# Low products on VectorE alone, and an eviction that runs key by key, in the spreading of the experts' weights of a PEER block

## The chip, the cores and the metric

One NeuronCore of a Trainium2 chip runs the whole program. The metric is the device time of one execution in microseconds; three executions of the kernel before gave 1767.48, 1770.31 and 1774.57 us, a median of 1770.31 us. The engines are TensorE (PE, with its weight loads PEld), VectorE (DVE), ScalarE (ACT), GpSimd (POOL) and the DMA queue of SyncE (SP). Each engine takes its instructions in the order in which they stand in its queue and waits on semaphores for the others.

## The reference, cut to what matters

The program is one decoder block: a token mixer (gated MLP and window attention), and then PEER, a layer that picks experts out of 128 x 128 = 16384 single-neuron experts. For each of 512 tokens and 8 heads it takes the 16 best pairs of a first and a second key, a softmax over their scores, and sums the chosen experts:

```python
e = (take_along_axis(i1, ci // 16) * 128 + take_along_axis(i2, ci % 16))
g = softmax(sc)
act = gelu(einsum('thkd,td->thk', peer_u[e], xb))
return einsum('thk,thkd->td', g * act, peer_v[e])
```

A token thus has 8 x 16 = 128 picks, each with a first key, a second key and a weight g.

## The kernel before, in words

For the first 384 tokens (three blocks of 128; `DENSE = 3`) the kernel computes all 16384 experts densely instead of gathering them: a U chunk is the product of the tokens with 128 experts' rows of `peer_u` (`U_chunk`, 128 chunks of 24 matmuls of 128x384: 8 slices of the model width times three products of hi and lo parts, lines 63 to 65), followed by GELU; a V chunk multiplies the activations by the experts' weights and by rows of `peer_v` and adds into six PSUM banks (lines 776 to 780). The weights must therefore stand as a full table: for every token a 128 x 128 matrix G[second key, first key], nearly all zeros. Making that table is the spreading (`spread`, lines 603 to 656), and it is the stage that the change touches.

`spread` goes over the three blocks of 128 tokens and, in each, over 8 groups of 16 tokens (`TG = 16`), 24 groups in all. At the start of a block three PE transposes (line 616) bring the picks' keys and weights into columns, ACT copies the keys to `iT` (line 618), and ACT and DVE cut the weights, times 32768, into a high and a low fp16 part `gT` (lines 620 and 621). For one group:

- DVE writes two one-hot tables of 128 x (16 tokens x 128 keys) in fp16: `oh[0]` for the second key (line 634) and `oh[1]` for the first key (line 635).
- The low product, `oh[1]` times the low part of the weights, goes to `oh[2]`: DVE makes it for 12 of the 16 tokens in one instruction (line 638), ACT for the other 4 (`NACT = 4`), one instruction a token with the weight as a per-partition scale from `gl`, an fp32 copy of the low part (lines 623, 624 and 640).
- The high product, `oh[1]` times the high part, is written over `oh[1]` itself by DVE (line 642). It can't start before every reader of the old `oh[1]` is done, ACT's four included.
- PE makes each token's 128 x 128 matrix with two matmuls (lines 650 and 651), four tokens to one PSUM bank `psg` (five such banks).
- ACT evicts each bank to the staging tile `stg` (line 652). `stg` holds [key i, token t] with t innermost, 16 tokens to a key. The bank holds [token, key]. Before, the instruction walks token by token: it reads the bank straight through and writes with a step of 16 floats.
- SP writes `stg` to memory, 1 MB (line 654).

`oh`, `stg`, `iT` and `gT` have two buffers each. The spreading runs beside U chunks: the main loop issues a U chunk and then lets about 5 us of background work be issued (`pump`, by fixed costs given to `yield`), which is close to one group a chunk. The tile framework puts the instructions of each engine in an order of its own when the program is built; that order is then fixed. A U chunk brings to ACT one split of the incoming rows (`hiU`, line 451) and one GELU (line 695), and to DVE one subtraction (`loU`, line 459).

After the spreading the dense V chunks run to the end, with the gather for the last 128 tokens beside them on POOL and DVE.

Of the kernel before, what the change touches and what calls it, by code (L numbers as in the profile page):

```python
# [8 lines left out]
F32 = mybir.dt.float32  # L9
# [4 lines left out]
AF = mybir.ActivationFunctionType  # L14
ALU = mybir.AluOpType
AX = mybir.AxisListType

P = 128
# [9 lines left out]
TG = 16  # L28
# [12 lines left out]
GR = 1.1  # L41
NACT = 4
NEV = 8
# [12 lines left out]
def block_kernel(ctx, tc, I, out):  # L56
    nc = tc.nc
# [52 lines left out]
    with ExitStack() as fr:  # L110
# [22 lines left out]

# [1 line left out]
        cs = wp.tile([P, D], F32, name="cs")  # L135
# [23 lines left out]

        # the first column blocks of the projection build up while the modulation comes in  # L160
        wf4 = Split(big(fp, "C", "w4hi"), big(fp, "D", "w4lo"))
# [15 lines left out]
        first = [I["w_k"], I["w_v"], I["w_q"][0], I["w_q"][1]]  # L177
# [21 lines left out]

# [1 line left out]
        att = ExitStack()  # L201
# [19 lines left out]

        # keys j of a block: those of the block itself where j <= q, those of the one before where j > q
        mcur = ap_.tile([P, P], F32, name="mcur")
# [66 lines left out]

# [1 line left out]
        vln = fp.tile([P, NT, D], F32, name="vln", tag="F", bufs=1)  # L292
# [12 lines left out]
        att.close()  # L305
# [1 line left out]
        sp_ = ExitStack()  # L307
# [32 lines left out]

# [1 line left out]
        gp = fr.enter_context(tc.tile_pool(name="gp", bufs=1, reuse_waits="tile"))  # L342
        part = big(keep, "E", "part", F32)
        for j in range(NK):
# [3 lines left out]
            for i in range(16 + 4 * j, 20 + 4 * j):  # L348
# [10 lines left out]
                   gp.tile([P, NK, S], F32R, name="mTlo"))  # L359
        # rows of 1 + gt1, 1 + gt2 and h2's scale and shift: turned, then spread to all partitions by DMA  # L360
        m4 = gp.tile([P, 4, NK], F32, name="m4")
# [24 lines left out]

# [1 line left out]
        xhat = keep.tile([P, NT, D], F32, name="xhat", tag="E", bufs=1)  # L388
# [10 lines left out]
        for hh in range(2):  # L399
            for t in range(NT):  # L400
# [13 lines left out]
                for kh in range(2):  # L414
# [15 lines left out]
                    nc.vector.tensor_sub(h2T.lo[dst], hf, h2T.hi[dst].bitcast(F32))  # L430
# [1 line left out]
    pw = ctx.enter_context(tc.tile_pool(name="pw", bufs=1, reuse_waits="tile"))  # L432
# [5 lines left out]
    def behind(ins, other):  # L438
        """keeps ins behind other in the queue of their engine"""
        tc.add_manual_dep(ins.ins, other.ins.name,  # L440
                          mybir.DependencyInfo(mybir.DependencyClass.NoSync, mybir.DependencyReason.DATA))
# [24 lines left out]

    # background work on the vector engine, given out in portions beside the dense products
    bg = []
# [10 lines left out]

# [1 line left out]
    def raw_row(nm):  # L481
# [18 lines left out]

# [1 line left out]
    tk = ExitStack()  # L502
# [34 lines left out]
    def topk(nm, n, src, dst):  # L537
        """src(half, j): the scores of lane j of n; dst(tensor): where the lanes' 16 choices go"""
        def tl(what, shape, dt):
            return tp.tile(shape, dt, name=f"{what}{nm}", tag=f"{what}_{n}", bufs=2 if n == DENSE else 1)  # L540
        v = [tl(f"v{i}", [P, n, 16], F32) for i in range(2)]
        ix = [tl(f"ix{i}", [P, n, 16], U32) for i in range(2)]
        for half in range(2):
            for j in range(n):
                top16(v[half][:, j, :], ix[half][:, j, :], src(half, j), P, f"{nm}{half}{j}")
                yield 1.02
        # candidates (a, b) in order; a pair outside the rows has 16 or more before it that are no smaller
        cand = tl("cand", [P, n, 17, 8], F32)
        nc.vector.tensor_tensor(cand[:, :, 0:2, :].rearrange("p t a b -> p t (a b)"), v[1],
                                v[0][:, :, 0:1].to_broadcast([P, n, 16]), op=ALU.add)  # L550
        nc.vector.tensor_tensor(cand[:, :, 2:17, :], v[0][:, :, 1:16].unsqueeze(3).to_broadcast([P, n, 15, 8]),
                                v[1][:, :, 0:8].unsqueeze(2).to_broadcast([P, n, 15, 8]), op=ALU.add)
        yield 0.12 + 0.14 * n
        sc = dst(scs)
        pos = tl("pos", [P, n, 16], U32)
        for j in range(n):
            top16(sc[:, j, :], pos[:, j, :], cand[:, j].rearrange("p a b -> p (a b)"), 136, f"c{nm}{j}")
            yield 1.06
        # positions to (a, b), then the keys they stand for
        r = tl("r", [P, n, 16], U32)  # L560
        ab = [tl(f"ab{i}", [P, n, 16], F16) for i in range(2)]
        nc.vector.tensor_scalar(r, pos, 3, None, op0=ALU.logical_shift_right)
        nc.vector.tensor_scalar(ab[0], r, 1, 0, op0=ALU.subtract, op1=ALU.max)
        nc.vector.scalar_tensor_tensor(ab[1], ab[0], 1.0, ab[0], op0=ALU.min, op1=ALU.add)
        nc.vector.scalar_tensor_tensor(ab[1], ab[1], -8.0, pos, op0=ALU.mult, op1=ALU.add)
        yield 0.4
        for i, to in ((0, i1s), (1, i2s)):
            ixf = tl("ixf", [P, n, 16], F16)
            nc.vector.tensor_copy(ixf, ix[i])
            oh = tl("ohl", [P, 16, n * 16], F16)  # L570
            nc.vector.tensor_tensor(oh, io16[:, :, 0:16 * n],
                                    ab[i].rearrange("p t k -> p (t k)").unsqueeze(1).to_broadcast([P, 16, 16 * n]),
                                    op=ALU.is_equal)
            o4 = oh.rearrange("p j (t k) -> p j t k", t=n)
            nc.vector.tensor_mul(o4, o4, ixf.rearrange("p t j -> p j t").unsqueeze(3).to_broadcast([P, 16, n, 16]))
            yield 0.2 + 0.42 * n
            for m in (8, 4, 2):
                nc.vector.tensor_add(oh[:, 0:m, :], oh[:, 0:m, :], oh[:, m:2 * m, :])
            nc.vector.tensor_add(dst(to), oh[:, 0, :].rearrange("p (t k) -> p t k", t=n),
                                 oh[:, 1, :].rearrange("p (t k) -> p t k", t=n))  # L580
            yield 0.2 + 0.14 * n
# [20 lines left out]

# [1 line left out]
    def spread():  # L604
# [8 lines left out]
        for t in range(DENSE):  # L613
            pt = pg.tile([P, 3, P], F32, name=f"ptg{t}", tag="ptg", bufs=1)
            for i, src in enumerate((i1s, i2s, gs)):
# [6 lines left out]
                                           op1=ALU.subtract)  # L622
            gl = gpool.tile([P, P], F32, name=f"gl{t}", tag="gl", bufs=2)
            nc.vector.tensor_copy(gl, gT[:, 1, :])
            yield 0.4
            for q in range(P // TG):
# [9 lines left out]
                yield 2.3  # L636
                nv = TG - NACT
                nc.vector.tensor_tensor(oh[2][:, 0:nv // 2], oh[1][:, 0:nv // 2], tok(gT[:, 1, :], nv), op=ALU.mult)
                for k in range(nv, TG):
                    nc.scalar.activation(oh[2][:, k // 2, :, k % 2], oh[1][:, k // 2, :, k % 2], AF.Copy,  # L640
                                         scale=gl[:, q * TG + k:q * TG + k + 1])
                nc.vector.tensor_tensor(oh[1], oh[1], tok(gT[:, 0, :]), op=ALU.mult)  # L642
                yield 2.3
                stg = gpool.tile([P, NCH, TG], F32, name=f"stg{nm}", tag="stg", bufs=2)
                for b in range(TG // 4):
                    ps = pg.tile([P, 4, P], F32, name=f"psg{nm}_{b}", tag="psg", bufs=5)
                    for i in range(4):
                        k = 4 * b + i
                        sel = (slice(None), k // 2, slice(None), k % 2)
                        nc.tensor.matmul(ps[:, i, :], oh[0][sel], oh[1][sel], start=True, stop=False)  # L650
                        nc.tensor.matmul(ps[:, i, :], oh[0][sel], oh[2][sel], start=False, stop=True)
                    nc.scalar.activation(stg[:, :, 4 * b:4 * b + 4].rearrange("p i t -> p t i"), ps, AF.Copy,  # L652
                                         scale=1.0 / 32768.0)
# [3 lines left out]

# [1 line left out]
    wg = gat.tile([P, P], F32, name="wg")  # L659
# [83 lines left out]
    def load_G(run):  # L743
        """weights for a run of at most 8 neighbouring chunks"""
        g = vs["vp"].tile([P, SD // TG, 8, TG], F32, name=f"G{run[0]}", tag="G", bufs=2)
        for lo, hi in ((0, 16), (16, 22), (22, 24)) if not gcur else ((0, 24),):
            nc.sync.dma_start(g[:, lo:hi, 0:len(run), :],
                              Gd[lo:hi, :, run[0]:run[-1] + 1, :].rearrange("g p i t -> p g i t"))
        for j, i in enumerate(run):
            gcur[i] = g[:, :, j, :]  # L750
# [210 lines left out]
```

## Time and profile before

| | us |
|---|---|
| median of three executions | 1770.31 |
| the profiled execution, first to last instruction (span) | 1769.1 |
| TensorE busy in it | 1666.7 |
| VectorE, ScalarE, GpSimd busy | 1342.3, 751.4, 450.3 |
| stretch from DVE's first one-hot to its last high product | 711.45 to 874.28 |

The page cuts the span into 40 slices of 44 us and gives each engine's busy share in tenths. The stretch of the spreading covers slices 16 to 19 (counted from 0: 708 to 884 us). A wait is shown where an engine stood idle and names the instruction whose end released it.

### The profile page before, as it was taken

The page shows a single profiled execution, that of the slowest core. Times are in us where ns is not written, and L with a number is a line of the kernel's source. Part 1 is how long each engine was busy: PE and PEld are TensorE (multiplying, and loading weights), DVE is VectorE, ACT ScalarE, POOL GpSimd, SP SyncE. Part 2 cuts the span into 40 slices and gives each one's busy share as a digit, 9 for nine tenths or more (in the row PEclk, how much of TensorE's full clock was granted, in tenths as well). Part 3 has the DMA queues.
Part 4 walks back from the last instruction along what each step waited for, and adds up shares of the span by engine and source line. Part 5 has one row for each costly group of instructions (what it writes and reads, how often), then busy time and mean ns, then how long its engine had stood idle before and what let it go on. Part 6 is the DMA issues. An engine that isn't in the chain of part 4 may idle for free.

```text
span 1769.1 us, 23554 instructions
## 1 busy us (share of the span) xinstructions
PE 1666.7 (94%) x8658; PEld 1444.7 (82%) x8658; DVE 1342.3 (76%) x2483; ACT 751.4 (42%) x1171; POOL 450.3 (25%) x321
## 2 busy tenths in 40 slices
PE   5999989999999991888999999999999999999997
PEld 3866778788788991788898899999999999999886
DVE  6466786444469999787978777878878878888776
ACT  3467632233523330888843333333333333333343
POOL 2000000000133541000012444444454554554002
PEclk9999999999999995999999999999999999999999
DMA  7502267542332341656799999999989989999972
GB/s 269 189 1 72 103 217 245 190 149 83 108 104 84 131 156 35 240 211 224 257 337 334 349 319 335 349 313 343 343 305 334 356 310 347 324 322 358 296 236 76
DMA packets 164837, 413.82 MB, mean 234 GB/s; under 512 B 24849, under 2 KB 75313, under 8 KB 161394
## 3 DMA queue, kind: packets, MB, share of 16 engines
q1 hardware_dynamic: 127330, 277.79, 45.7%
q0 software_dynamic: 36960, 134.50, 21.3%
q8 instruction: 67, 1.10, 0.2%
q14 instruction: 48, 0.39, 0.1%
q10 hardware_dynamic: 432, 0.04, 0.0%
HBM read 379.04 MB, written 32.98 MB: 233 GB/s over the span
## 4 chain that ended last, share of the span: by engine, by line
PE 46%; issue 2%; DVE 1%; ACT 1%; POOL 1%; DMA 0%; DVEq 0%; POOLq 0%; ACTq 0%
PE acc L779 9%; PE acc L780 9%; PE acc L776 9%; PE psU L65 7%; PE psU L63 7%; PE psU L64 7%; ACT stg L652 1%; POOL ru L665 1%; DMA ru<-in_peer_u_dram,idx 0%; ACT oh L640 0%; DVE oh L642 0%; DVE xhat L707 0%; DVE oh L635 0%; DVE xhat L715 0%; DVE ru L667 0%
## 5 line engine op out<-in xcount | busy, mean ns | idle before, releaser
L65 PE MATMUL psU<-h2Thi,loU 128*128 128x384 f32 x1008 | 340.1, 337 | 38.0 <-DVE loU L459 38.0
L63 PE MATMUL psU<-h2Thi,hiU 128*128 128x384 f32 x1008 | 340.5, 338 | 0.0
L64 PE MATMUL psU<-h2Tlo,hiU 128*128 128x384 f32 x1008 | 339.7, 337 | 0.0
L780 PE MATMUL acc<-hiV,wl 128*128 128x512 f32 x768 | 300.3, 391 | 0.0
L779 PE MATMUL acc<-loV,wh 128*128 128x512 f32 x768 | 300.1, 391 | 0.0
L776 PE MATMUL acc<-hiV,wh 128*128 128x512 f32 x768 | 298.6, 389 | 1.2 <-ACT wh L761 1.2
L665 POOL DMA_INDIRECT ru<-in_peer_u_dram,idx x128 | 155.5, 1215 | 466.3 <-DVE ru L667 410.2
L459 DVE TENSOR_TENSOR loV<-rawV,hiV 128x1024 fp32r<-128x1024 f32 x128 | 156.6, 1224 | 117.1 <-ACT hiV L451 116.9
L451 ACT ACTIVATE hiV<-rawV 128x1024 fp32r<-128x1024 f32 x128 | 135.3, 1057 | 242.1 <-PE psU L64 224.2
L676 POOL DMA_INDIRECT rv<-in_peer_v_dram,idx x128 | 181.9, 1421 | 209.1 <-DVE facc L682 185.7
L65 PEld LDWEIGHTS psU<-h2Thi,loU 128*128 128x128 f32 x1008 | 190.5, 189 | 38.3 <-DVE loU L459 38.3
L451 ACT ACTIVATE hiU<-rawU 128x1024 fp32r<-128x1024 f32 x126 | 133.7, 1062 | 169.6 <-PE acc L780 75.2
L64 PEld LDWEIGHTS psU<-h2Tlo,hiU 128*128 128x128 f32 x1008 | 190.7, 189 | 3.0
L63 PEld LDWEIGHTS psU<-h2Thi,hiU 128*128 128x128 f32 x1008 | 190.5, 189 | 3.0
L780 PEld LDWEIGHTS acc<-hiV,wl 128*128 128x128 f32 x768 | 144.1, 188 | 30.4 <-DVE wl L762 0.3
L776 PEld LDWEIGHTS acc<-hiV,wh 128*128 128x128 f32 x768 | 144.2, 188 | 29.8 <-ACT wh L761 1.5
L779 PEld LDWEIGHTS acc<-loV,wh 128*128 128x128 f32 x768 | 144.1, 188 | 28.7 <-DVE loV L459 0.3
L682 DVE SCALAR_TENSOR_TENSOR facc<-rv,wg,facc 128x1024 f32<-128x1024 f32 x126 | 159.3, 1279 | 9.5 <-DMA rv<-in_peer_v_dram,idx 9.3
L761 ACT ACTIVATE wh<-wf 128x384 fp32r<-128x384 f32 x128 | 67.1, 526 | 216.3 <-DVE wf L757 112.8
L667 DVE SCALAR_TENSOR_TENSOR ru<-ru,h2n 128x1024 f32<-128x1024 f32 x128 | 154.3, 1221 | 5.6 <-DMA ru<-in_peer_u_dram,idx 5.6
L459 DVE TENSOR_TENSOR loU<-rawU,hiU 128x1024 fp32r<-128x1024 f32 x108 | 131.5, 1220 | 5.7 <-ACT hiU L451 5.7
L457 POOL TENSOR_TENSOR lopq<-rawpq,hipq 128x1024 fp32r<-128x1024 f32 x16 | 39.2, 2452 | 323.2 <-ACT hipq L451 323.2
(626 smaller groups left out, 2946.5 us busy)
## 6 DMA issues: line engine op xcount, KB each, us to landing
rawU<-in_uT_dram SPq DMA_DIRECT2D x128, 512.0 KB, 5.0
rawV<-in_peer_v_dram SPq DMA_DIRECT2D x128, 512.0 KB, 6.0
wa<-in_w_ada_dram SPq DMA_DIRECT2D x48, 512.0 KB, 4.3
Gd<-stg SPq DMA_DIRECT2D x24, 1024.0 KB, 3.9
G<-Gd SPq DMA_DIRECT2D x13, 1536.0 KB, 14.6
rawpq<-in_w_pq_dram SPq DMA_DIRECT2D x16, 512.0 KB, 3.7
Ad<-act SPq DMA_DIRECT2D x29, 192.0 KB, 2.8
ar<-Ad SPq DMA_DIRECT2D x7, 768.0 KB, 7.7
```

The source lines that it names most:

```text
L63: nc.tensor.matmul(ps, l.hi, r.hi, start=(i == 0), stop=False)
L64: nc.tensor.matmul(ps, l.hi, r.lo, start=False, stop=False)
L65: last = nc.tensor.matmul(ps, l.lo, r.hi, start=False, stop=(i == n - 1))
L451: h = nc.scalar.activation(hi, raw, AF.Copy)
L459: last["dve"] = nc.vector.tensor_sub(lo, raw, hi.bitcast(F32))
L665: nc.gpsimd.indirect_dma_start(out=rows, out_offset=None, in_=I["peer_u"], in_offset=bass.IndirectOffsetOnAxis(ap=idx[:, s:s + 1], axis=0))
L667: paced(nc.vector.scalar_tensor_tensor(rows, rows, 1.0, h2n, op0=ALU.mult, op1=ALU.mult, accum_out=wg[:, s:s + 1]))
L676: nc.gpsimd.indirect_dma_start(out=rows, out_offset=None, in_=I["peer_v"], in_offset=bass.IndirectOffsetOnAxis(ap=idx[:, s:s + 1], axis=0))
L682: paced(nc.vector.scalar_tensor_tensor(fa, rows, wg[:, s:s + 1], fa, op0=ALU.mult, op1=ALU.add))
L776: m = nc.tensor.matmul(acc, l.hi, r.hi, start=st, stop=False)
L779: nc.tensor.matmul(acc, l.hi, r.lo, start=False, stop=False)
L780: nc.tensor.matmul(acc, l.lo, r.hi, start=False, stop=sp_)
```

## The change: what it does

`oh[2]` is made by one DVE instruction for all 16 tokens; ACT's four instructions, the copy `gl` and `NACT` are gone. The eviction has the same 512 elements, the same bank and the same place in `stg`, but the loops are exchanged: for each key it takes four tokens, so that it reads the bank with a step of 128 floats and writes four neighbouring floats at a time. Costs at `yield` are as they were. Comments are removed too, so line numbers are lower by one and, behind the edit, by up to seven.

```diff
-NACT = 4
...
-            gl = gpool.tile([P, P], F32, name=f"gl{t}", tag="gl", bufs=2)
-            nc.vector.tensor_copy(gl, gT[:, 1, :])
             yield 0.4
...
                 yield 2.3
-                nv = TG - NACT
-                nc.vector.tensor_tensor(oh[2][:, 0:nv // 2], oh[1][:, 0:nv // 2], tok(gT[:, 1, :], nv), op=ALU.mult)
-                for k in range(nv, TG):
-                    nc.scalar.activation(oh[2][:, k // 2, :, k % 2], oh[1][:, k // 2, :, k % 2], AF.Copy,
-                                         scale=gl[:, q * TG + k:q * TG + k + 1])
+                nc.vector.tensor_tensor(oh[2], oh[1], tok(gT[:, 1, :]), op=ALU.mult)
                 nc.vector.tensor_tensor(oh[1], oh[1], tok(gT[:, 0, :]), op=ALU.mult)
                 yield 2.3
...
-                    nc.scalar.activation(stg[:, :, 4 * b:4 * b + 4].rearrange("p i t -> p t i"), ps, AF.Copy,
+                    nc.scalar.activation(stg[:, :, 4 * b:4 * b + 4], ps.rearrange("p t i -> p i t"), AF.Copy,
                                          scale=1.0 / 32768.0)
```

VectorE's order in the middle of the first block, before; `oh_0_5` is a one-hot or product tile of block 0, group 5, and the line tells which (634 and 635 the tables, 638 the low product, 642 the high one):

```order
L638 TENSOR_TENSOR oh_0_5_6025<-oh_0_5_6024,gT_5593 128x1536
L634 TENSOR_TENSOR oh_0_6_6108<-io,iT_5591 128x2048
L642 TENSOR_TENSOR oh_0_5_6024<-oh_0_5_6024,gT_5593 128x2048
L635 TENSOR_TENSOR oh_0_6_6109<-io,iT_5591 128x2048
L459 TENSOR_TENSOR loU_6388<-rawU_6385,hiU_6387 128x1024
```

The same place now (lines 631 and 632 the tables, 634 the low product, 635 the high one):

```order
L634 TENSOR_TENSOR oh_0_5_6003<-oh_0_5_6002,gT_5593 128x2048
L631 TENSOR_TENSOR oh_0_6_6082<-io,iT_5591 128x2048
L635 TENSOR_TENSOR oh_0_5_6002<-oh_0_5_6002,gT_5593 128x2048
L632 TENSOR_TENSOR oh_0_6_6083<-io,iT_5591 128x2048
L458 TENSOR_TENSOR loU_6344<-rawU_6341,hiU_6343 128x1024
```

The five instructions stand in the same order; the low product has grown from 1536 to 2048 elements.

ScalarE's order around the evictions of group 4, before; `stg_4<-psg_4_0` is the eviction of bank 0 of group 4, `oh_0_5` with `gl` a low product of the group behind it:

```order
L652 ACTIVATE stg_4_5981<-psg_4_0_5982 128x4x128
L640 ACTIVATE oh_0_5_6025<-oh_0_5_6024,gl_5596 128x128
L652 ACTIVATE stg_4_5981<-psg_4_1_5992 128x4x128
L652 ACTIVATE stg_4_5981<-psg_4_2_6002 128x4x128
L652 ACTIVATE stg_4_5981<-psg_4_3_6012 128x4x128
L640 ACTIVATE oh_0_5_6025<-oh_0_5_6024,gl_5596 128x128 x3
L451 ACTIVATE hiU_6387<-rawU_6385 128x1024
L695 ACTIVATE res<-psU_6125 128x384
```

And now:

```order
L645 ACTIVATE stg_4_5959<-psg_4_0_5960 128x128x4
L645 ACTIVATE stg_4_5959<-psg_4_1_5970 128x128x4
L645 ACTIVATE stg_4_5959<-psg_4_2_5980 128x128x4
L645 ACTIVATE stg_4_5959<-psg_4_3_5990 128x128x4
L450 ACTIVATE hiU_6343<-rawU_6341 128x1024
L688 ACTIVATE res<-psU_6095 128x384
```

The low products are gone from between and behind the evictions, and the eviction's free sizes are 128 x 4 where they were 4 x 128.

ScalarE's order at the change from the second block to the third, before; `iT` and `gT` are the columns that the third block's one-hots and products need:

```order
L652 ACTIVATE stg_6_6842<-psg_6_3_6873 128x4x128
L652 ACTIVATE stg_7_6895<-psg_7_0_6896 128x4x128
L652 ACTIVATE stg_7_6895<-psg_7_1_6906 128x4x128
L652 ACTIVATE stg_7_6895<-psg_7_2_6916 128x4x128
L652 ACTIVATE stg_7_6895<-psg_7_3_6926 128x4x128
L618 CAST iT_6941<-ptg_6937 128x256
L620 ACTIVATE gT_6943<-ptg_6937 128x128
```

And now:

```order
L645 ACTIVATE stg_6_6778<-psg_6_3_6809 128x128x4
L617 CAST iT_6873<-ptg_6869 128x256
L619 ACTIVATE gT_6875<-ptg_6869 128x128
L645 ACTIVATE stg_7_6827<-psg_7_0_6828 128x128x4
```

The third block's keys and weights now stand ahead of group 7's four evictions. On PE the transposes that feed them moved ahead of group 7's matmuls in the same way. The spreading's matmuls keep their order among themselves; 8 matmuls of a U chunk moved ahead of the first group. Nothing moved on POOL, and on SP a few neighbouring transfers changed places. Behind the spreading PE's order is the same.

## Rows read from the trace of the kernel before

**Rows 1.** The page: span, busy time by engine, and two lines of slices
```profile
span 1769.1 us, 23554 instructions
...
PE 1666.7 (94%) x8658; PEld 1444.7 (82%) x8658; DVE 1342.3 (76%) x2483; ACT 751.4 (42%) x1171; POOL 450.3 (25%) x321
...
PE   5999989999999991888999999999999999999997
...
PEclk9999999999999995999999999999999999999999
```
**Rows 2.** Windows: length, busy PE, PEld, DVE, ACT, POOL, then clock, DMA
```profile
711.50:874.35 162.85, 139.48 (x1255) 133.09 (x1254) 133.03 (x127) 141.74 (x236) 0.00 (x0) 0.98 0.61 227
717.20:876.40 159.20, 135.83 (x1254) 129.54 (x1253) 129.38 (x122) 140.53 (x232) 0.00 (x0) 0.98 0.61 226
```
**Rows 3.** Waits in 711.4 to 876.4 us: total, times, longest
```profile
PE psg L650 <- DVE oh L642: 23.0, 17, 2.6
DVE oh L642 <- ACT oh L640: 22.4, 16, 3.4
...
DVE oh L634 <- ACT iT L618: 6.5, 2, 5.7
...
DVE oh L635 <- PE psg L650: 1.1, 1, 1.1
```
**Rows 4.** Timeline of DVE from 744 us: start, length, line, idle before in brackets
```profile
746.94 0.95 DVE L638 TENSOR_TENSOR oh<-oh,gT 128x1536 f16<-128x1536 f16 x1
747.81 1.22 DVE L634 TENSOR_TENSOR oh<-io,iT 128x2048 f16<-128x2048 f16 x1
750.41 1.23 DVE L642 TENSOR_TENSOR oh<-oh,gT 128x2048 f16<-128x2048 f16 x1 [1.38 <-ACT oh L640]
751.55 1.22 DVE L635 TENSOR_TENSOR oh<-io,iT 128x2048 f16<-128x2048 f16 x1
752.69 1.22 DVE L459 TENSOR_TENSOR loU<-rawU,hiU 128x1024 fp32r<-128x1024 f32 x1
...
757.29 1.23 DVE L642 TENSOR_TENSOR oh<-oh,gT 128x2048 f16<-128x2048 f16 x1 [1.38 <-ACT oh L640]
```
**Rows 5.** Timeline of ACT in the same period
```profile
746.68 2.92 ACT L652 ACTIVATE stg<-psg 128x512 f32<-128x512 f32 x3
749.36 1.02 ACT L640 ACTIVATE oh<-oh,gl 128x128 f16<-128x128 f16 x3
750.21 1.07 ACT L451 ACTIVATE hiU<-rawU 128x1024 fp32r<-128x1024 f32 x1
751.16 0.51 ACT L695 ACTIVATE res<-psU 128x384 f32<-128x384 f32 x1
752.41 2.95 ACT L652 ACTIVATE stg<-psg 128x512 f32<-128x512 f32 x3 [0.75 <-ACT res L695]
```
**Rows 6.** Timeline of PE in the same period
```profile
751.69 0.23 PE L650 MATMUL psg<-oh,oh 128*128 128x128 f16 x1 [1.52 <-DVE oh L642]
```
**Rows 7.** Timeline at the change to the third block, ACT, then DVE
```profile
813.26 7.29 ACT L652 ACTIVATE stg<-psg 128x512 f32<-128x512 f32 x8
820.35 0.40 ACT L618 CAST iT<-ptg 128x256 f16<-128x256 f32 x1
...
820.78 1.22 DVE L634 TENSOR_TENSOR oh<-io,iT 128x2048 f16<-128x2048 f16 x1 [5.66 <-ACT iT L618]
```
**Rows 8.** DVE's groups by shape, 711.4 to 874.4 us: busy, mean ns
```profile
L642 DVE TENSOR_TENSOR oh<-oh,gT 128x2048 f16<-128x2048 f16 x24 | 29.4, 1224 | 22.5 <-ACT oh L640 22.4
...
L638 DVE TENSOR_TENSOR oh<-oh,gT 128x1536 f16<-128x1536 f16 x24 | 22.9, 952 | 0.0
...
L624 DVE CAST gl<-gT 128x128 f32<-128x128 f16 x3 | 0.7, 221 | 0.0
```
**Rows 9.** ACT's groups by shape, whole span, two of 512 elements from PSUM
```profile
L652 ACT ACTIVATE stg<-psg 128x512 f32<-128x512 f32 x96 | 93.3, 1117 | 11.9 <-ACT res L695 3.8 <-issue 3.6 <-ACT hiU L451 2.6
...
L527 ACT COPY sall<-pssc 128x512 f32<-128x512 f32 x16 | 9.5, 591 | 0.0
```
**Rows 10.** Windows behind the spreading, columns as in Rows 2
```profile
900.00:1100.00 200.00, 198.78 (x958) 174.56 (x958) 159.55 (x233) 70.79 (x93) 74.23 (x62) 1.00 0.97 337
```

## The prediction

> **What bounds the kernel now.** I read the page first. TensorE is busy for 94% of the span, and in the slices it stands at nine tenths or more nearly everywhere, but not in slices 16 to 18, where the spreading runs and it stands at eight [rows 1]. So the change can only win what PE idles there, and I read that stretch by itself. In the 159.2 us from its first to its last matmul of the spreading, PE is busy for 135.8: 23.4 us idle [rows 2]. Behind it PE is busy for 198.8 of 200 us [rows 10], so what the stretch gives back reaches the end nearly one to one.
>
> Next I asked who waits for whom. PE waits 23.0 us in 17 waits for VectorE's high product (L642), and that product waits 22.4 us in 16 waits for ScalarE's low products (L640) [rows 3]. VectorE is the head: in its 162.85 us it works 133.0 [rows 2], and the 29.8 it idles are nearly all named, 22.4 for L640 and 6.5 for `iT` [rows 3].
>
> Why ScalarE is late is seen in one period. A high product starts at 750.41, the next at 757.29: 6.88 us [rows 4]. The first ends at about 751.64 and PE starts its group at 751.69 [rows 6]; ScalarE starts the evictions at 752.41, and only behind them come the next group's low products, which the next high product waits for [rows 5]. It is a ring: low product, high product, matmuls, evictions, low product. ScalarE is busy for 141.7 of the 162.85 us [rows 2] and idles just where it waits for the ring (0.75 us [rows 5]).
>
> **The change part by part.** *Low products to VectorE.* The new instruction has the shape and operands of the high product, 2048 elements, 1224 ns, against 952 for 1536 [rows 8]. Neighbouring starts are 1.14 us apart for 2048 elements (750.41, 751.55, 752.69) and 0.87 for 1536 (746.94, 747.81) [rows 4]: 0.27 more, by 24 groups, +6.5 us on VectorE, which is on the path. The copy `gl` goes: 3 x 0.22 [rows 8], -0.7.
>
> *The ring is cut.* VectorE's high product no longer waits for any ScalarE instruction. Of the 22.4 us [rows 3] nothing is left by that route: -22.4.
>
> *The change of block.* `iT` of the third block stood behind eight evictions, 813.26 to 820.35, and VectorE waited 5.66 us for it [rows 7]. It now stands ahead of group 7's four. From the end of group 6's high product, `iT` is ready after 0.8 us to the first eviction (751.64 to 752.41 [rows 5, 6]), four evictions at 0.89 ((820.35 - 813.26)/8 [rows 7]) and 0.4 for itself, 4.8 us. VectorE has four instructions of 1.14 to do first, 4.6 us. About 0.2 to 0.5 us of wait remains: -5.2. If the eviction gets cheaper it vanishes.
>
> *ScalarE.* It loses 96 low products. What it keeps is four evictions, one split (0.95 us, 750.21 to 751.16) and one GELU (0.5) a period [rows 5]. With evictions at today's spacing of 0.89 that is 3.55 + 0.95 + 0.5 = 5.0 us, under VectorE's new period of five instructions of 1.14, 5.7 us. So ScalarE's work is hidden by VectorE's, and the eviction's own time counts for nothing as long as it stays under (5.7 - 1.45)/4 = 1.06 us of spacing. Duration and spacing differ by 0.23 us (1117 ns [rows 9] against 0.89), so that is a duration of 1.29 us.
>
> *The eviction's time* isn't shown by the trace: nothing in it reads PSUM by steps of 512 bytes. From below: 512 elements read and written straight through take 591 ns [rows 9]; lower it can't be, since the element count is the same. Today's write, one float every 64 bytes, costs 1117: the step is worth 0.53 us. The new write goes in runs of four floats, and I take its penalty as gone. The new read has the step instead. If a stepped read costs what the stepped write costs, the eviction stays at 1.12; if reads are insensitive, it is 0.6. From above: both penalties at once, 0.59 + 2 x 0.53 = 1.65. I take 0.6 to 1.12, and the sum is the same at either end.
>
> [...]
>
> *PE.* It isn't given less work. VectorE's account is -22.4 - 5.2 - 0.7 + 6.5 = -21.8 us, but PE has only 23.4 us idle to give [rows 2], and it would be left with 1.6 us of slack in some 137. Two engines that feed each other through double buffers, one at 5.7 us a period and the other only a little under it, will not fit so closely. Today VectorE waits 1.1 us for PE to free a one-hot buffer [rows 3], with all that slack. For such waits I charge 5 us, between 0 and half of the wait that goes, 11. The granted clock, 0.98 in this stretch [rows 2], gives PE up to 3 us more if it stays full.
>
> **The sum** is -21.8 + 5 = -16.8 us. The profiled span of 1769.1 becomes 1752; it lies 1.2 us under the median of 1770.3, so the forecast is 1753.5 us. With the charge's two ends, 0 and 11: 1748.5 and 1759.5.
>
> **Rivals.** *A: the stepped read is dear, and ScalarE paces the stretch.* For: nothing in the trace shows such a read, and ScalarE was the busiest engine here. Against: it has 1.9 us a period to spare against today's 6.88. Its place is the four evictions; it decides from a duration of 1.29 us, where ScalarE's period passes VectorE's. At 1.59 us (spacing 1.36) the old period of 6.88 is back, and at 1.68 the kernel is slower by more than 0.5%. At both penalties at once, 1.65 us, the period is 4 x 1.42 + 1.45 = 7.13, +0.25 x 24 = +6: 1776, not yet told from no change. With a read penalty two and a half times the write's, 0.59 + 2.5 x 0.53 = 1.92 us, the period is 4 x 1.69 + 1.45 = 8.2, +1.33 x 24 = +32: 1802 us.
>
> *B: PE becomes the bound.* For: its 23.4 us of idle time is only a little more than VectorE's account. Then VectorE's waits for free buffers eat nothing but its own time, the stretch is packed, and with the clock's 3 us up to 25 are won: 1746. Against: VectorE still makes every group just before PE needs it.
>
> *C: half of the gain goes back into new waits.* With a period of 5.7 us the split `hiU` sits behind four evictions on ScalarE, and VectorE's `loU` behind it; one late split stops VectorE's whole queue, and PE's U chunk with it. For: at evictions of 1.12 us ScalarE's 5.0 us leave 0.7 to spare. Against: the split is for a chunk that PE takes up a whole group later. Half of 16.8 gives 1762.
>
> *D: the time is given back behind the stretch,* since the DMA engines are 97% busy there [rows 10]. Against: PE hardly waits there, and the transfers' order relative to PE's work is what it was. It would give 1766 to 1770.
>
> **Chances.** The forecast, with B as its lower end, 0.74; C 0.08; D 0.05; A 0.13, of which 0.09 slower and 0.04 near no change. A measurement of this kernel tells about 0.5% from no change, 8.9 us: faster means under 1761.5, slower over 1779. Faster is the forecast and half of C, 0.78; same the other half of C, D and a third of A, 0.13; slower the rest of A, 0.09. The likeliest case's own range is 1746 to 1760; to leave out 2 in 10 or less the range is 1745 to 1768, which takes in C and part of D.
>
> **What would show it.** In the new profile no wait of VectorE for a ScalarE product may be left, the `iT` wait should be under 1 us, the low product should take 1.22 us, and high products should stand about 5.7 us apart where a U chunk lies between. ScalarE should be well under 141.7 us in the stretch, with evictions between 0.6 and 1.12 us. From VectorE's first one-hot to its last high product there should be about 146 us in place of 162.8, and the rest of the program should be as long as before. It is wrong if the eviction takes over 1.3 us, if VectorE shows many waits for PE or for splits, or if PE's time behind the stretch grows.

## The result, and the profile after

The changed kernel takes 1745.2 us (median of 4 runs, 1740.98 to 1746.54) against 1770.55 for the kernel before (1767.48 to 1774.57). The ratio is 0.9859, 95% interval 0.9844 to 0.9873: 1.4% faster, 25 us where 16.8 were forecast. The profiled execution has a span of 1744.8 us.

The page of the changed kernel, the lines that answer to [rows 1]; slices 16 to 18 have gone from eight tenths of PE's time to nine:

```profile
PE 1661.5 (95%) x8658; PEld 1440.6 (83%) x8658; DVE 1346.3 (77%) x2480; ACT 685.9 (39%) x1075; POOL 448.7 (26%) x321
...
PE   6999989999999991999999999999999999999997
```

Windows of the changed kernel, columns as in [rows 2], first from VectorE's first one-hot to its last high product, then from PE's first to its last matmul of the spreading:

```profile
709.65:845.65 136.00, 134.92 (x1251) 129.25 (x1250) 135.96 (x123) 77.86 (x139) 0.00 (x0) 1.00 0.75 268
716.80:848.25 131.45, 130.37 (x1246) 124.66 (x1245) 131.41 (x118) 75.93 (x136) 0.00 (x0) 1.00 0.76 273
```

VectorE's stretch went from 162.85 to 136.0 us, and it works through all of it. PE's went from 159.2 to 131.45, and of 23.4 us idle 1.1 are left: both engines are now full. ScalarE's busy time there fell from 141.7 to 77.9.

Waits of the changed kernel in the same stretch, answering to [rows 3]:

```profile
PEld L643 <- DVE oh L635: 5.9, 19, 0.6
DVE oh L631 <- ACT iT L617: 0.8, 1, 0.8
...
PE psg L643 <- DVE oh L635: 0.6, 2, 0.3
```

No wait of VectorE for a ScalarE product is left, nor one for PE. The 0.8 us for `iT` are the first block's, at the start of the stretch; the third block's 5.66 [rows 7] are gone. PE's 23.0 us for the high product became 0.6. Its weight loads still wait for that product, 5.9 us in 19 pieces, mostly hidden under matmuls still running: VectorE remains the engine that releases PE, by a hair.

Timeline of VectorE and then ScalarE in one period of the changed kernel, answering to [rows 4, 5]:

```profile
741.66 1.21 DVE L631 TENSOR_TENSOR oh<-io,iT 128x2048 f16<-128x2048 f16 x1
742.79 1.21 DVE L635 TENSOR_TENSOR oh<-oh,gT 128x2048 f16<-128x2048 f16 x1
...
748.47 1.21 DVE L635 TENSOR_TENSOR oh<-oh,gT 128x2048 f16<-128x2048 f16 x1
```
```profile
742.86 0.47 ACT L688 ACTIVATE res<-psU 128x384 f32<-128x384 f32 x1
744.78 2.07 ACT L645 ACTIVATE stg<-psg 128x512 f32<-128x512 f32 x4 [1.45 <-issue]
748.26 1.06 ACT L450 ACTIVATE hiU<-rawU 128x1024 fp32r<-128x1024 f32 x1 [1.42 <-PE psU L63]
```

High products stand 5.68 us apart, where they stood 6.88, and four evictions take 2.07 us where three took 2.92 [rows 5]. ScalarE now idles between the groups' evictions.

The groups of the low product and of the eviction, answering to [rows 8, 9]; the first number behind the bar is the busy time, the second the mean in ns:

```profile
L634 DVE TENSOR_TENSOR oh<-oh,gT 128x2048 f16<-128x2048 f16 x24 | 29.1, 1213 | 0.0
```
```profile
L645 ACT ACTIVATE stg<-psg 128x512 f32<-128x512 f32 x96 | 49.5, 605 | 24.7 <-issue 12.9 <-PE psg L644 10.3 <-ACT res L688 1.2
```

The eviction fell from 1117 to 605 ns, near the lower end of the forecast's bounds and of the 591 ns of a straight read and write [rows 9].

Behind the stretch this execution of the changed kernel loses a little: from PE's last matmul of the spreading to the end it takes 896.55 us (1744.8 - 848.25) where it took 892.7 (1769.1 - 876.4). The one wait of PE there, after and then before:

```profile
PE acc L769 <- ACT wh L754: 3.8, 1, 3.8
```
```profile
PE acc L776 <- ACT wh L761: 1.2, 1, 1.2
```

### The profile page after: what moved, and what is told of

Its sections match the earlier page's. It is cut to its first block, busy times and chain, and to the rows that moved or that the text cites. A ratio compares the mean times of both kernels' runs of the same rounds, so it can differ in the third digit from the quotient of the medians.

```text
span 1744.8 us, 23426 instructions
## 1 busy us (share of the span) xinstructions
PE 1661.5 (95%) x8658; PEld 1440.6 (83%) x8658; DVE 1346.3 (77%) x2480; ACT 685.9 (39%) x1075; POOL 448.7 (26%) x321
## 4 chain that ended last, share of the span: by engine, by line
PE 62%; DVE 17%; DMA 3%; issue 3%; POOL 1%; ACT 0%; DVEq 0%; POOLq 0%; ACTq 0%
PE acc L772 9%; PE acc L773 9%; PE acc L769 9%; PE psU L64 8%; PE psU L62 8%; PE psU L63 8%; DMA wa<-in_w_ada_dram 2%; DMA rawV<-in_peer_v_dram 1%; DVE oh L632 1%; DVE oh L635 1%; DVE loU L458 1%; DVE oh L634 1%; PE pso L62 1%; PE pso L63 1%; PE pso L64 1%
## 5 line engine op out<-in xcount | busy, mean ns | idle before, releaser
L675 DVE SCALAR_TENSOR_TENSOR facc<-rv,wg,facc 128x1024 f32<-128x1024 f32 x126 | 159.2, 1278 | 13.4 <-DMA rv<-in_peer_v_dram,idx 13.4
```

Of the source, the lines that this page charges most:

```text
L675: paced(nc.vector.scalar_tensor_tensor(fa, rows, wg[:, s:s + 1], fa, op0=ALU.mult, op1=ALU.add))
```

## The experiments

**The ring alone, with the old eviction.**

```diff
-                    nc.scalar.activation(stg[:, :, 4 * b:4 * b + 4], ps.rearrange("p t i -> p i t"), AF.Copy,
+                    nc.scalar.activation(stg[:, :, 4 * b:4 * b + 4].rearrange("p i t -> p t i"), ps, AF.Copy,
```

> The changed kernel with the old eviction (token by token, written with a step of 16 floats); all low products stay on VectorE. Theory, the ring is what cost the time: VectorE no longer waits for ScalarE, and ScalarE's period of 4 x 0.89 + 1.45 = 5.0 us lies under VectorE's 5.68, so the eviction stays at 1.12 us and is hidden; the stretch from VectorE's first one-hot to its last high product is 136 to 139 us and the time within 0.5% of the changed kernel's, 1741 to 1751 us. Rival, the cheaper eviction is what won the time: the time comes back at least half way, to 1758 us or more, and VectorE or PE shows waits for evictions.

Measured: 1746.16 us (5 runs, 1744.19 to 1751.82), 0.9873 of the kernel before, interval 0.9856 to 0.989. Its eviction's group, two waits of VectorE and its stretch:

```profile
L645 ACT ACTIVATE stg<-psg 128x512 f32<-128x512 f32 x96 | 92.4, 1129 | 10.8 <-ACT res L688 3.7 <-issue 2.9 <-PE psg L644 2.5
```
```profile
DVE gT L620 <- ACT gT L619: 1.0, 1, 1.0
DVE oh L631 <- ACT iT L617: 0.8, 1, 0.8
```
```profile
711.00:848.00 137.00, 134.92 (x1251) 129.12 (x1250) 135.95 (x123) 115.48 (x139) 0.00 (x0) 1.00 0.71 267
```

The eviction takes 1129 ns, nearly twice the changed kernel's, and the stretch is 137 us in place of 136. The theory held: with the ring cut the eviction's time is hidden but for one wait of 1.0 us for `gT` at a change of block, and low products on VectorE alone give the gain. The third block's `iT` wait is also gone here, so it did not need the cheaper eviction.

**The eviction alone,** in the kernel before, with four low products of a group still on ScalarE.

```diff
-                    nc.scalar.activation(stg[:, :, 4 * b:4 * b + 4].rearrange("p i t -> p t i"), ps, AF.Copy,
+                    nc.scalar.activation(stg[:, :, 4 * b:4 * b + 4], ps.rearrange("p t i -> p i t"), AF.Copy,
```

> The kernel before with the new eviction alone; ScalarE still makes four low products of a group. Theory: the ring stays, but its evictions shrink from 3.55 to about 2.0 us, so that it turns in about 1.2 (high product) + 0.75 (to the first eviction) + 2.0 + 1.0 (low products) = 5.0 us, under VectorE's own 5.4 (four instructions of 1.14 and one of 0.87); waits of VectorE for low products fall from 22.4 to under 5 us, PE is full in the stretch and the time is within 0.5% of the changed kernel's, 1738 to 1752 us: either part would have done. Rival, low products on ScalarE are late whatever the eviction costs, because they stand in its queue behind splits and GELUs: the waits stay at half or more and the time at 1757 us or more.

Measured: 1742.46 us (4 runs, 1741.81 to 1744.09), 0.9852, interval 0.9837 to 0.9867. Its waits of VectorE for ScalarE, its VectorE stretch, and VectorE and then PE at the change to the third block:

```profile
DVE oh L634 <- ACT iT L618: 3.3, 2, 2.4
...
DVE oh L642 <- ACT oh L640: 2.3, 2, 1.9
```
```profile
709.30:845.80 136.50, 135.25 (x1252) 129.58 (x1251) 131.47 (x127) 105.19 (x235) 0.00 (x0) 1.00 0.73 268
```
```profile
799.83 1.22 DVE L634 TENSOR_TENSOR oh<-io,iT 128x2048 f16<-128x2048 f16 x1 [2.42 <-ACT iT L618]
```
```profile
798.38 0.27 PE L616 MATMUL ptg<-ident,gs 128*128 128x128 f32 x1
```

The ring still stands, but with cheap evictions (601 ns each) it turns faster than VectorE works, and the wait for low products falls from 22.4 to 2.3 us. So either part alone gives the whole gain, and together they give no more. The window says why. VectorE has 4.5 us less to do than in the changed kernel (131.47 against 135.96) and idles 5.0, yet the stretch is no shorter: PE is busy for 135.25 of 136.5 us, so a VectorE with less to do has little to win. Of the 5.0 us, 2.4 are the wait for the third block's `iT`: PE is through with its transposes only at 798.65 us, in the middle of that wait. PE's work fills the stretch in both kernels; in the changed kernel VectorE's fills it too.

**Single writes,** to tell the read from the write: the four tokens of a bank are put 4 apart in `stg`, so that floats are written singly, 16 bytes apart, with the read as in the changed kernel.

```diff
-                        k = 4 * b + i
+                        k = 4 * i + b
...
-                    nc.scalar.activation(stg[:, :, 4 * b:4 * b + 4], ps.rearrange("p t i -> p i t"), AF.Copy,
+                    nc.scalar.activation(stg[:, :, b:TG:4], ps.rearrange("p t i -> p i t"), AF.Copy,
```

> The changed kernel with the four tokens of a bank 4 apart in stg: the eviction reads PSUM by the same steps of 512 bytes but writes single floats 16 bytes apart instead of runs of four. [...] Rival, only the length of the old step (64 bytes) was dear: about 0.6 to 0.7 us.

Measured: 1744.76 us (4 runs, 1744.13 to 1745.63), 0.9861, interval 0.9846 to 0.9876.

```profile
L645 ACT ACTIVATE stg<-psg 128x512 f32<-128x512 f32 x96 | 93.7, 1146 | 10.1 <-ACT res L688 3.4 <-issue 2.9 <-PE psg L644 2.4
```

The read steps as in the changed kernel and the eviction is dear again, 1146 ns where that kernel's takes 605: what the old form paid for is the write of single floats, dear at steps of 16 bytes here and at 64 in the first experiment (1129 ns), so the rival fell. Writing runs of four and reading by steps of 512 bytes cost at most 14 ns together, 605 ns against 591 for the straight read and write [rows 9]. The time stayed: 1744.76 us against 1745.2.

**Three evictions of each bank,** to price a slow eviction (rival A).

```diff
-                    nc.scalar.activation(stg[:, :, 4 * b:4 * b + 4], ps.rearrange("p t i -> p i t"), AF.Copy,
-                                         scale=1.0 / 32768.0)
+                    for _ in range(3):
+                        nc.scalar.activation(stg[:, :, 4 * b:4 * b + 4], ps.rearrange("p t i -> p i t"), AF.Copy,
+                                             scale=1.0 / 32768.0)
```

> The changed kernel with each bank evicted three times to the same place. Theory, ScalarE paces the stretch once its period passes VectorE's: 12 x 0.49 + 1.45 = 7.3 us against 5.68, so 24 groups cost 1.65 x 24 = 40 us more, and the change of block some 5 more where the order puts the third block's keys behind a group's evictions: 1780 to 1795 us, slower than the kernel before. Rival, PSUM buffers and ScalarE's idle time hide most of it: under 1765 us.

Measured: 1796.47 us (4 runs, 1792.2 to 1799.68), 1.0152 of the kernel before, interval 1.0133 to 1.0172. The eviction's group, the waits from 705 to 905 us, and VectorE's stretch:

```profile
L646 ACT ACTIVATE stg<-psg 128x512 f32<-128x512 f32 x288 | 148.0, 821 | 1.1 <-PE psg L644 1.1
```
```profile
DVE loU L458 <- ACT hiU L450: 21.3, 10, 6.4
...
PE psg L643 <- ACT stg L646: 14.2, 11, 2.2
...
DVE oh L632 <- PE psg L643: 12.5, 9, 4.5
...
DVE oh L631 <- ACT iT L617: 6.3, 2, 5.5
```
```profile
709.70:879.30 169.60, 143.12 (x1173) 131.35 (x1172) 134.14 (x118) 154.34 (x306) 0.00 (x0) 0.90 0.51 195
```

At 0.51 us of ScalarE per eviction (148.0/288) the period is 12 x 0.51 + 1.45 = 7.6 us, and 24 x (7.6 - 5.68) + 5.5 for `iT` is 51.6 us; measured were 51.3 over the changed kernel's 1745.2. The time lay just over the range that I had set, which used 0.49. That the sum comes so near is in part luck: in the trace VectorE's stretch is 33.6 us longer (169.6 against 136.0), the rest of the time is lost behind it, and ScalarE is busy for 154.34 of the 169.6 us, not for all. VectorE's largest waits here are for splits of U chunks (21.3 us), which the sum doesn't have. So rival A was a real danger of about the right price: what kept it away is that the eviction stayed under the break-even, which the forecast estimated at 1.29 us: it takes 605 ns in the changed kernel and 1129 and 1146 in the first and third experiments.

**Two low products on ScalarE,** with the new eviction, and the changed kernel itself once more beside it. The edit to the kernel of the second experiment:

```diff
-NACT = 4
+NACT = 2
```

> The new eviction, and two low products of a group on ScalarE instead of four or none. Theory, PE fills the stretch in every version whose engines keep under its pace, so moving low products between VectorE and ScalarE moves nothing: PE idles 1 to 2 us in the stretch and the time is within 0.3% of the changed kernel's run beside it. Rival, VectorE is the bound in the changed kernel: each two products taken from it give about 2 to 3 us (24 x 0.13 = 3).

> The changed kernel itself beside the others on one chip. Every theory: 0.986 of the kernel before, about 1745 us. If the wait of PE for the first V chunk behind the G load (3.8 us at 971 us in its first trace, 1.2 before) is a steady cost of the earlier end of the stretch it is there again at 3 to 4 us; if it is chance it is anywhere from 0 to 4.

Measured: 1744.88 us (6 runs, 1742.34 to 1752.9), 0.9858, interval 0.9833 to 0.9883; the changed kernel 1742.6 (5 runs, 1741.35 to 1746.34), 0.9845, interval 0.9822 to 0.9868. Two, four or no low products on ScalarE can't be told apart, so no version beats the changed kernel beyond measurement. The version with two products, from PE's first to its last matmul of the spreading:

```profile
713.40:846.95 133.55, 131.97 (x1255) 126.26 (x1254) 129.79 (x121) 88.94 (x182) 0.00 (x0) 1.00 0.74 268
```

VectorE has 3.8 us to spare and PE idles 1.6, as expected: VectorE's work is not what keeps the time from falling further. PE's wait behind the stretch, first in the version with two products, then in the changed kernel's second trace:

```profile
PE acc L776 <- ACT wh L761: 7.2, 1, 7.2
```
```profile
PE acc L769 <- ACT wh L754: 0.2, 1, 0.2
```

The same program shows 3.8 us in one trace and 0.2 in the other, so this wait is chance and no steady price of the earlier end. The single runs differ by as much. In that second trace PE's last matmul of the spreading ends at 850.7, and what follows takes 891.7 us (1742.4 - 850.7), no more than the 892.7 before. Its stretch:

```profile
719.15:850.70 131.55, 130.45 (x1247) 124.66 (x1246) 131.51 (x119) 75.22 (x135) 0.00 (x0) 1.00 0.75 269
```

**One buffer** for each one-hot and product tile, to see what lets two nearly full engines run side by side.

```diff
-                oh = [gpool.tile(shp, F16, name=f"oh{i}_{nm}", tag=f"oh{i}", bufs=2) for i in range(3)]
+                oh = [gpool.tile(shp, F16, name=f"oh{i}_{nm}", tag=f"oh{i}", bufs=1) for i in range(3)]
```

> The changed kernel with one buffer instead of two for each one-hot and product tile, to see what keeps VectorE and PE from waiting for each other. Theory, it is the second buffer: with one, VectorE's next first-key table waits until PE is through with the group, about 2.0 us behind each high product, so the period is 5.68 + 2.0 where no U chunk's split lies between, and the time rises by up to 24 x 2.0 = 48 us: 1775 to 1795. Rival, VectorE finds other work to put there (splits of U chunks, 1.14 us each), and PE's queue was never the reason: under 1762.

Measured: 1783.08 us (4 runs, 1782.43 to 1788.38), 1.008, interval 1.0052 to 1.0108.

```profile
DVE oh L632 <- PE psg L643: 25.8, 17, 3.6
PE psg L643 <- DVE oh L635: 21.1, 6, 5.4
```
```profile
715.90:903.00 187.10, 165.82 (x1418) 160.50 (x1417) 154.45 (x138) 89.86 (x155) 3.55 (x3) 0.93 0.66 238
```
```profile
PE acc L769 <- ACT wh L754: 13.1, 2, 12.9
```

VectorE waits for PE 17 times in the 24 groups and PE for VectorE in turn; with two buffers both waits are under 1 us. So it is the second buffer that keeps them from waiting for each other, not a lack of load. The time is 40 us over the changed kernel beside it, within the range that I had set, but not all of it is these waits: PE idles 21.3 us in its stretch, where it idled 1.1, and 13.1 us behind it, in the wait that differs between traces of one program; how much of that is chance isn't shown. The granted clock is 0.93 in the stretch, where it was 1.00.

## Why the prediction was right, and where its size was off

**What held the stretch up** was right: the ring of low product, high product, matmuls and evictions. Cutting it at the low product (first experiment) or shortening it at the evictions (second) each gave the gain.

**The terms.** The wait for ScalarE's low products, -22.4 forecast, is gone entirely. The `iT` wait fell by 5.7 (6.5 to 0.8) where 5.2 were forecast: at the third block nothing is left of it. The low products grew by 6.2 us (22.9 to 29.1) where 6.5 were. VectorE's stretch is 136.0 us where the forecast meant about 146. It shrank by 26.85 us: 22.4 + 5.7 + 1.5 of waits for PE, less 6.2, plus 0.7 for `gl`, are 24.1; one `xhat` product of 1.2 us that stood inside the stretch now stands behind it, and 1.5 remain that these rows don't separate.

**The step that was mis-sized** is the charge: "two engines that feed each other through double buffers ... will not fit so closely ... for such waits I charge 5 us". It measured nothing. VectorE waits for PE nowhere, and PE idles 1.1 us in 131.45. The last experiment shows that the reason I gave is a reason only without the second buffer. The changed kernel ended at the time of rival B, which I had kept as the forecast's lower end: 1746 forecast, 1745.2 measured. B's mechanism came only half: PE is full, and the second and fifth experiments show that a lighter VectorE wins nothing more; but VectorE, which by B would wait for free buffers, works all the time and waits for PE nowhere. The two are level. Against B I had said that VectorE would make every group just before PE needs it; it makes most of them a little after (the 19 waits of PE's weight loads), and it hardly matters, since PE idles 1.1 us by it.

The charge and the clock are most of the 8 us between forecast and result. PE's busy time in its stretch also fell, by 5.5 us (135.83 to 130.37): 1.4 are the 8 matmuls that moved ahead of the first group (8 x 0.173), and most of the rest goes with the granted clock, 1.00 in the stretch where it was 0.98 (an estimate: 0.02 x 159 = 3.2). The forecast named the clock and didn't put it into the sum.

**The eviction** was bounded rightly, 0.6 to 1.12 us, and so was the claim that the sum is the same at either end: the changed kernel has the one end, the first and third experiments the other, and their times agree within 0.2%. The forecast took the penalty of the write as gone with runs of four, and the three write patterns bear it out: 1129 ns for single floats at steps of 64 bytes, 1146 at 16, 605 in runs of four. What the forecast left open was the read. Stepping by 512 bytes costs ScalarE nearly nothing in this kernel, 605 ns against 591.

**Rivals.** A fell to the eviction's 605 ns, and the fourth experiment bears out its price in the whole, though not term by term. C (new waits eat half) fell: a wait of `loU` for a split isn't in the changed kernel's stretch at all; it appears in the fourth experiment, where ScalarE has too much to do. D, and with it the forecast's sign that PE's time behind the stretch must not grow, was met in the first trace: 3.9 us more, of which 2.6 are PE's wait (3.8 against 1.2). The second trace of the same program has neither, so it is chance.

**The range** was too tight at its lower end. The first measurement lies at its edge (1745.2 against 1745.0), and the changed kernel's second, 1742.6, is below it; that the first fell inside is luck. The floor of 1746 for B took 25 us as the most that could be won. PE's stretch alone shrank by 27.7 us in both traces: 22.3 us of idle time, and some 5.4 of busy time (1.4 of them moved ahead of it) where the clock had been put at 3.

## What to carry to other kernels

Where engines hand work to each other, look for the ring and add up one turn of it. The engine with the highest busy share may only be a part of the ring; here cutting the ring and shortening its longest piece gave the same gain, and gave it once. The next bound then takes over, so add up every engine's own work a period before adding gains: here VectorE's 5.68 us and PE's idle 23.4 us capped whatever ScalarE gave back. Before charging for two nearly full engines that work side by side, look at the buffers between them: in this kernel the charge was nothing with two and some 20 us of PE's time with one.

## What the runs showed of the hardware

Walking a transposition so that the stepping falls on the PSUM read and the SBUF write goes in runs of 16 bytes nearly halves ScalarE's eviction in this kernel: 605 ns for 512 floats, where single floats at steps of 64 or 16 bytes take 1117 to 1146.

In the stretch before, PE's two longest idle times, 2.62 us each, were followed by a granted clock of 0.50. PE's timeline there, the idle time in brackets:

```profile
784.46 0.23 PE L650 MATMUL psg<-oh,oh 128*128 128x128 f16 x1 [2.62 <-DVE oh L642]
...
826.67 0.22 PE L650 MATMUL psg<-oh,oh 128*128 128x128 f16 x1 [2.62 <-DVE oh L642]
```

Windows around them, the first with one microsecond of it, and then the first window in the changed kernel:

```profile
780.00:790.00 10.00, 7.38 (x55) 7.07 (x54) 7.41 (x7) 9.25 (x18) 0.00 (x0) 0.83 0.68 237
786.00:787.00 1.00, 1.00 (x10) 1.00 (x8) 1.00 (x2) 1.00 (x3) 0.00 (x0) 0.50 0.87 332
820.00:830.00 10.00, 7.38 (x57) 7.15 (x55) 8.97 (x10) 5.83 (x13) 0.00 (x0) 0.84 0.32 125
```
```profile
780.00:790.00 10.00, 10.00 (x96) 9.45 (x95) 10.00 (x10) 5.40 (x10) 0.00 (x0) 1.00 0.81 284
```

At 786 us PE was busy again and the granted clock was 0.50; in windows of one microsecond it is 0.50 from 786 to 789 us and from 827 to 830, lies between 0.88 and 0.92 in the microsecond to either side, and is 1.00 in the rest of the stretch. Other single idle times of PE in that stretch, 1.78 us at most, were not followed by it. In the changed kernel PE was busy throughout the same 10 us and the clock stayed at 1.00. By the mean clocks of 0.83 and 0.84, the lower clock behind the two waits cost PE an estimated 1.7 and 1.6 us of work besides their own length, together about the 3.2 us that the stretch's 0.98 gives.
